# Differential attention's score rows combined by GpSimd in two operations, not by VectorE in one

## The chip, the core and the metric

The kernel runs on one core of a Trainium2 chip. The core has five engines, each with its own queue of instructions that it takes strictly in order: TensorE (PE in the profile; its weight loads are PEld), VectorE (DVE), ScalarE (ACT), GpSimd (POOL) and SyncE (SP), which issues most DMAs. They meet through semaphores. The metric is the device time of one execution in microseconds (us).

## The reference, cut to what matters

The program is a backbone of two layers over 1024 latent tokens and 256 context tokens, width 1024, float32. Each layer normalizes its input, projects it into four groups of heads (a state-space mixer, an mLSTM, differential attention, gated linear attention), joins them by an output projection and adds a squared-ReLU MLP. The change lies in differential attention. Each of its 4 heads makes two maps of scores; their softmaxes are subtracted, with a learned factor lam, before the values are summed:

```
s = einsum('bqhmd,bkhmd->bhmqk', qb, keys)      # m = 0, 1: two score maps
pr = softmax(s, axis=-1)
w = pr[:, :, 0] - lam * pr[:, :, 1]
return einsum('bhqk,bkhv->bqhv', w, vals)
```

Queries are latent tokens against all 1280 keys, and, in the first layer only, context tokens against the 256 context keys.

## The kernel before

The attention is a generator, `da_mix` (lines 453 to 594). It works on blocks of 128 queries, which I call score rows: 8 per head over 1280 keys, and in layer 0 also 2 per head over 256 keys. That is 40 score rows in layer 0 and 32 in layer 1. For one score row:

- `scores` (line 478) takes the map m = 1 first and then m = 0. Per map TensorE makes up to three pieces of scores, of 512, 512 and 256 keys (line 488, tile daps in PSUM). VectorE copies each piece to SBUF with its sign turned and takes its minimum in the same instruction (line 489, tile das). Line 498 joins the three minima. ScalarE makes the exponentials in place and their sum (line 500).
- The SBUF tile of a map has its own tag: two buffers for m = 1 and four for m = 0 (line 483, `bufs=4 - 2 * m`).
- `combine` (line 503) makes a factor r1 of 128x1 (lines 506 and 507: -lam times the sum of map 0 over the sum of map 1) and then S0 + r1 * S1 in place of S0 (line 508). It is put off: the list `late` runs it when the third score piece of the next row has been laid out (line 490).
- `values` (line 513) takes two score rows at a time: TensorE transposes blocks of the combined S0 into PSUM (line 529, tile dapt), ScalarE copies them to SBUF (line 530), and TensorE multiplies them with the values (line 520, tile dapo). `finish` (line 540) normalizes and writes the head's result to DRAM (tile mix).

Line 1497 of the main function mixes three such generators: the attention, a quarter as many steps of the mLSTM (`ml_mix`, lines 694 to 884), and the first half of the output projection (`p_out`, line 1467). In `p_out` ScalarE scales a PSUM result (line 1481, tile pg, one buffer) and GpSimd adds it to the residual (line 1482, tile xo). Lines 1446 and 1458 are VectorE's share of splitting operands into a high and a low part, lines 767, 771, 812, 839 and 853 VectorE's or GpSimd's share of the mLSTM. The transposes of the attention and the output projection share two PSUM banks in this stage (line 1487, `wo="b", dat="b"`).

The order in which an engine gets its instructions is not the order of the code: the framework lays the whole program out ahead by its own estimates, and adds the semaphore waits that the tiles ask for. A change in one instruction can so move others on every engine.

Of the kernel before, what the change touches and what calls it, by code (L numbers as in the profile page):

```python
# [17 lines left out]
ALU = mybir.AluOpType  # L18
# [434 lines left out]
def da_mix(env, l, st, V, lamv, lam_init, normg, bones, out_cb, need_ctx):  # L453
# [4 lines left out]
    v, g, act, pe = nc.vector, nc.gpsimd, nc.scalar, nc.tensor  # L458
    with tc.tile_pool(name=f"dam{l}", bufs=1, reuse_waits="tile") as P:
# [18 lines left out]
        def scores(Q, K, qt, k1, rs):  # L478
            S, sm = {}, {}
            late_at = 2  # L480
            npc = (k1 + 511) // 512
            for m in (1, 0):
                s = S[m] = P.tile([128, T], F32, tag="s%d" % m, name="das", bufs=4 - 2 * m)
                pm = P.tile([128, 4], F32, tag="pm", name="dapm", bufs=6)
                for i in range(npc):
                    a, b = 512 * i, min(k1, 512 * i + 512)
                    p = env.bank("das2" if i == 2 else "das", "daps")
                    pe.matmul(p[:, 0:b - a], Q[m][:, 128 * qt:128 * qt + 128], K[m][:, a:b], start=True, stop=True)  # L488
                    v.tensor_scalar(s[:, a:b], p[:, 0:b - a], -1.0, None, op0=ALU.mult, op1=ALU.min, accum_out=pm[:, i:i + 1])  # L489
                    if not late_at:  # L490
                        while late:
                            late.pop(0)()
                    late_at -= 1
                    yield 1
                nm = pm
                if npc > 1:
                    nm = P.tile([128, 1], F32, tag="nm", name="danm", bufs=6)
                    v.tensor_reduce(nm, pm[:, 0:npc], axis=AX.X, op=ALU.min)  # L498
                sm[m] = P.tile([128, 1], F32, tag="sm", name="dasm", bufs=6) if m else rs
                act.activation(s[:, :k1], s[:, :k1], AF.Exp, bias=nm[:, 0:1], scale=-1.0, accum_out=sm[m])  # L500
            tiles.append(S[0])

            def combine():

                r1 = P.tile([128, 1], F32, tag="rs", name="dars", bufs=6)
                v.reciprocal(r1, sm[1])
                v.tensor_scalar(r1, r1, nlam, sm[0], op0=ALU.mult, op1=ALU.mult)
                v.scalar_tensor_tensor(S[0][:, :k1], S[1][:, :k1], r1, S[0][:, :k1], op0=ALU.mult, op1=ALU.add)
            late.append(combine)
            while len(late) > 1:  # L510
                late.pop(0)()
# [1202 lines left out]
```

## Time and profile before

| | us |
|---|---|
| median of 3 runs | 3652.22 (3648.07 to 3656.89) |
| profiled execution | 3661.21 |
| its span, first to last instruction | 3659.4 |
| TensorE busy / VectorE busy / GpSimd busy | 3389.7 / 2168.1 / 453.0 |
| mean granted clock of TensorE | 0.951 of full speed |

Busy shares are means over stages with different limits, so what bounds one stage is read from that stage's own stretch of time. The attention stage of layer 0 lies between 633 and 975 us from the span's start and that of layer 1 between 2550 and 2857 us. Idle time is put down to what ended it; where several instructions were awaited, to the one that came last by the profile.

### The profile page before, as it was taken

The numbers are of one execution on the slowest core, as the hardware profiler recorded it, in microseconds if no ns is written. First come the engines' busy times: TensorE is split into PE (matmuls) and PEld (weight loads), VectorE is DVE, ScalarE is ACT, GpSimd is POOL, SyncE is SP. The second block draws the span as 40 slices with busy tenths as digits, with TensorE's granted clock in tenths as the row PEclk, the third lists the DMA queues.
The fourth block names the chain that finished last, engine by engine and source line by source line (L and its number), as shares of the span: only waits on it lengthen the run. The fifth ranks groups of instructions, "written<-read, shape, count | busy, mean of one in ns | idle before, by whom it ended". The sixth has DMA issues, their size and how long they took to land. (4 is left out here: it accounts for less than half of the span.)

```text
span 3659.4 us, 58369 instructions
## 1 busy us (share of the span) xinstructions
PE 3389.7 (93%) x22794; PEld 2687.6 (73%) x22794; DVE 2168.1 (59%) x5431; ACT 1301.5 (36%) x2453; POOL 453.0 (12%) x520
## 2 busy tenths in 40 slices
PE   6999998898789999999999798988889899999998
PEld 3867767676657888888888476867676578888885
DVE  9664655888659855455554647465888443333334
ACT  4223435666542121212112522445676322222222
POOL 2131221223100000000000123131222000000000
PEclk8989988899899999999999899998999899999999
DMA  6674325655451222222111365315654511111112
GB/s 222 238 225 150 119 79 171 201 186 158 163 179 60 95 87 80 74 76 76 64 41 38 108 199 167 119 59 173 198 179 139 168 41 49 50 47 52 46 52 75
DMA packets 233977, 430.54 MB, mean 118 GB/s; under 512 B 47414, under 2 KB 135910, under 8 KB 233446
## 3 DMA queue, kind: packets, MB, share of 16 engines
q1 hardware_dynamic: 192806, 381.03, 32.0%
q10 hardware_dynamic: 35520, 30.52, 2.6%
q0 software_dynamic: 5376, 15.28, 1.2%
q8 instruction: 179, 2.93, 0.3%
q14 instruction: 96, 0.79, 0.1%
HBM read 316.88 MB, written 109.86 MB: 117 GB/s over the span
## 5 line engine op out<-in xcount | busy, mean ns | idle before, releaser
L1563 DVE SCALAR_TENSOR_TENSOR X<-m2p,mods,X 128x256 f32<-128x256 f32 (+1 forms) x512 | 345.4, 683 | 345.2 <-PE m2p L1127 344.7
L1116 ACT CAST whi<-raw 128x1024 fp32r<-128x1024 f32 x182 | 191.1, 1050 | 916.2 <-PE m2p L1126 634.9
L1125 PE MATMUL m2p<-hidhi,whi 128*128 128x512 f32 (+1 forms) x1280 | 473.5, 372 | 2.0 <-DVE X L1563 1.3
L1125 PE MATMUL m1p<-h2hi,whi 128*128 128x512 f32 (+1 forms) x1280 | 472.6, 370 | 0.2 <-ACT h2hi L1210 0.2
L1127 PE MATMUL m2p<-hidhi,wlo 128*128 128x512 f32 (+1 forms) x1280 | 471.9, 370 | 0.8 <-DVE wlo L1117 0.8
L1126 PE MATMUL m2p<-hidlo,whi 128*128 128x512 f32 (+1 forms) x1280 | 472.7, 369 | 0.0
L1126 PE MATMUL m1p<-h2lo,whi 128*128 128x512 f32 (+1 forms) x1280 | 471.0, 368 | 0.0
L1127 PE MATMUL m1p<-h2hi,wlo 128*128 128x512 f32 (+1 forms) x1280 | 470.9, 368 | 0.0
L1117 DVE TENSOR_TENSOR wlo<-raw,whi 128x1024 fp32r<-128x1024 f32 x182 | 224.6, 1234 | 321.8 <-ACT whi L1116 303.8
L1125 PEld LDWEIGHTS m2p<-hidhi,whi 128*128 128x128 f32 x1280 | 241.4, 189 | 59.1 <-issue 9.1
L1125 PEld LDWEIGHTS m1p<-h2hi,whi 128*128 128x128 f32 x1280 | 241.0, 188 | 46.4 <-ACT whi L1116 4.2
L1127 PEld LDWEIGHTS m2p<-hidhi,wlo 128*128 128x128 f32 x1280 | 241.0, 188 | 46.3 <-issue 3.4
L1126 PEld LDWEIGHTS m2p<-hidlo,whi 128*128 128x128 f32 x1280 | 241.4, 189 | 41.8 <-issue 2.2
L1126 PEld LDWEIGHTS m1p<-h2lo,whi 128*128 128x128 f32 x1280 | 241.2, 188 | 40.6 <-DVE h2lo L1211 0.7
L1127 PEld LDWEIGHTS m1p<-h2hi,wlo 128*128 128x128 f32 x1280 | 241.0, 188 | 40.3 <-issue 0.4
L1125 PE MATMUL zp<-hhi,whi 128*128 128x512 f32 (+1 forms) x664 | 258.8, 390 | 11.3 <-ACT zst L1238 9.6
L1126 PE MATMUL zp<-hlo,whi 128*128 128x512 f32 (+1 forms) x664 | 255.7, 385 | 8.6 <-DVE hlo L1206 8.1
L1127 PE MATMUL zp<-hhi,wlo 128*128 128x512 f32 (+1 forms) x664 | 255.9, 386 | 0.0
L489 DVE TENSOR_SCALAR_CACHE_REDUCE das<-daps 128x512 f32<-128x512 f32 (+1 forms) x400 | 226.4, 588 | 44.8 <-PE daps L488 42.2
L1577 DVE TENSOR_TENSOR rl<-rl,m1p 128x256 f32<-128x256 f32 (+1 forms) x160 | 100.8, 630 | 172.2 <-ACT rl L1576 172.0
L500 ACT ACTIVATE das<-das,danm 128x1280 f32<-128x1280 f32 x128 | 174.2, 1362 | 51.4 <-DVE danm L498 51.0
L1125 PE MATMUL zp<-whi,hhi 128*128 128x256 f32 x624 | 183.6, 295 | 5.4 <-ACT whi L1116 5.2
(459 smaller groups left out, 6483.6 us busy)
## 6 DMA issues: line engine op xcount, KB each, us to landing
raw<-w SPq DMA_DIRECT2D x136, 512.0 KB
adaw<-ada_w SPq DMA_DIRECT2D x96, 512.0 KB
whl<-wsp SPq DMA_DIRECT2D x80, 512.0 KB
wsp<-whl SPq DMA_DIRECT2D x32, 512.0 KB
raw<-wz SPq DMA_DIRECT2D x30, 512.0 KB
daqk<-da_st SPq DMA_DIRECT2D x24, 640.0 KB
mlE<-ml_rows SPq DMA_DIRECT2D x16, 640.0 KB
xn<-xo SPq DMA_DIRECT2D x72, 128.0 KB
```

What stands on the lines that cost most here:

```text
L489: v.tensor_scalar(s[:, a:b], p[:, 0:b - a], -1.0, None, op0=ALU.mult, op1=ALU.min, accum_out=pm[:, i:i + 1])
L500: act.activation(s[:, :k1], s[:, :k1], AF.Exp, bias=nm[:, 0:1], scale=-1.0, accum_out=sm[m])
L1116: nc.scalar.copy(hi, raw)
L1117: nc.vector.tensor_tensor(lo, raw, hi.bitcast(F32), op=ALU.subtract)
L1125: pe.matmul(out, ah, bh, start=i == 0, stop=False)
L1126: pe.matmul(out, ah, bl, start=False, stop=False)
L1127: pe.matmul(out, al, bh, start=False, stop=i == n - 1)
L1563: nc.vector.scalar_tensor_tensor(X[b][:, m], p[:, :n], mod(l, 5, s)[:, m:m + 1], X[b][:, m], op0=ALU.mult, op1=ALU.add)
L1577: nc.vector.tensor_tensor(rl[:, :n], rl[:, :n], p[:, :n], op=ALU.mult)
```

## The change

Line 508 is replaced by two instructions of GpSimd: the first multiplies S1 by r1 in place, the second adds it to S0. The factor r1 stays on VectorE. All lines behind move down by one (line 529 becomes 530, line 1446 becomes 1447, and so on).

```
                 v.reciprocal(r1, sm[1])
                 v.tensor_scalar(r1, r1, nlam, sm[0], op0=ALU.mult, op1=ALU.mult)
-                v.scalar_tensor_tensor(S[0][:, :k1], S[1][:, :k1], r1, S[0][:, :k1], op0=ALU.mult, op1=ALU.add)
+                g.tensor_scalar(S[1][:, :k1], S[1][:, :k1], r1, None, op0=ALU.mult)
+                g.tensor_tensor(S[0][:, :k1], S[0][:, :k1], S[1][:, :k1], op=ALU.add)
             late.append(combine)
```

The framework's order differs on all engines in the two stages. Three places follow; in the rows a name's number tells one tile from another, and a wait names the engine whose semaphore is awaited (DMAHW: a DMA).

First, GpSimd near the beginning of layer 0's attention stage, before:

```order
L1482 TENSOR_TENSOR xo_6965<-xo_6965,pg_6986 128x256 [waits DMAHW7_49,DMAHW4_49,Activation_49]
L1482 TENSOR_TENSOR xo_7068<-xo_7068,pg_7089 128x256 [waits DMAHW5_49,DMAHW1_49,Activation_49]
L1482 TENSOR_TENSOR xo_7176<-xo_7176,pg_7197 128x256 [waits DMAHW3_49,DMAHW1_49,Activation_49]
L1482 TENSOR_TENSOR xo_7275<-xo_7275,pg_7296 128x256 [waits DMAHW6_49,DMAHW3_49,Activation_49]
L1482 TENSOR_TENSOR xo_7376<-xo_7376,pg_7397 128x256 [waits DMAHW7_49,DMAHW1_49,Activation_49]
L1482 TENSOR_TENSOR xo_7463<-xo_7463,pg_7484 128x256 [waits DMAHW7_49,DMAHW5_49,Activation_49]
```

And with the change, at the same place:

```order
L1483 TENSOR_TENSOR xo_6968<-xo_6968,pg_6989 128x256 [waits DMAHW6_49,DMAHW3_49,Activation_49]
L768 TENSOR_TENSOR mlE_7261<-mlE_7261,mlcm_7002 128x1280 [waits DMAHW7_49]
L1483 TENSOR_TENSOR xo_7072<-xo_7072,pg_7093 128x256 [waits DMAHW5_49,DMAHW1_49,Activation_49]
L508 TENSOR_SCALAR das_7031<-das_7031,dars_7176 128x1280 [waits DVE_49]
L509 TENSOR_TENSOR das_7057<-das_7057,das_7031 128x1280 [waits PE_49,Pool_49]
L1483 TENSOR_TENSOR xo_7181<-xo_7181,pg_7202 128x256 [waits DMAHW3_49,DMAHW0_49,Activation_49]
L508 TENSOR_SCALAR das_7151<-das_7151,dars_7311 128x1280 [waits DVE_49]
L509 TENSOR_TENSOR das_7210<-das_7210,das_7151 128x1280 [waits PE_49,Activation_49,Pool_49]
L1483 TENSOR_TENSOR xo_7280<-xo_7280,pg_7301 128x256 [waits DMAHW7_49,DMAHW3_49,Activation_49]
L508 TENSOR_SCALAR das_7275<-das_7275,dars_7434 128x1280 [waits DVE_49]
L509 TENSOR_TENSOR das_7320<-das_7320,das_7275 128x1280 [waits PE_49,Pool_49]
```

GpSimd had the additions of line 1482 and now and then an operation of the mLSTM; now a pair of lines 508 and 509 stands between nearly every two of them, and waits for VectorE's line 507 (tile dars).

Second, VectorE in layer 0, around the factor of one score row, before:

```order
L507 TENSOR_SCALAR dars_7306<-dars_7306,nlam_6698,dark_6804 128x1 [waits DVE_49,Activation_49]
L791 SCALAR_TENSOR_TENSOR mlC_7320<-mlC_7320,mlal_6647,mlpu_7327 128x65 [waits PE_49]
L1458 TENSOR_TENSOR whl_7277<-raw_7278,whl_7277 128x512 [waits DMAHW5_49,DMAHW2_49,Activation_49]
L508 SCALAR_TENSOR_TENSOR das_7205<-das_7147,dars_7306,das_7205 128x1280 [waits DVE_49]
L489 TENSOR_SCALAR das_7314,dapm_7315<-daps_7334 128x256
L791 SCALAR_TENSOR_TENSOR mlC_7319<-mlC_7319,mlal_6647,mlpu_7354 128x65 [waits PE_49]
L498 TENSOR_REDUCE danm_7337<-dapm_7315 128x1 [waits DVE_49]
L791 SCALAR_TENSOR_TENSOR mlC_7320<-mlC_7320,mlal_6647,mlpu_7358 128x65 [waits PE_49]
L1458 TENSOR_TENSOR whl_7378<-raw_7379,whl_7378 128x512 [waits DMAHW6_49,DMAHW5_49,Activation_49]
L489 TENSOR_SCALAR das_7409,dapm_7410<-daps_7411 128x512
```

With the change:

```order
L507 TENSOR_SCALAR dars_7311<-dars_7311,nlam_6698,dark_6805 128x1 [waits Activation_49]
L498 TENSOR_REDUCE danm_7343<-dapm_7321 128x1 [waits DVE_49]
L489 TENSOR_SCALAR das_7415,dapm_7416<-daps_7417 128x512 [waits Pool_49]
L772 TENSOR_TENSOR mlkw_7221<-mlkn_7006,mlE_7261 128x10x64 [waits DMAHW7_49,Activation_49]
L1459 TENSOR_TENSOR whl_7282<-raw_7283,whl_7282 128x512 [waits DMAHW2_49,DMAHW1_49,Activation_49]
L792 SCALAR_TENSOR_TENSOR mlC_7326<-mlC_7326,mlal_6647,mlpu_7333 128x65 [waits PE_49]
L489 TENSOR_SCALAR das_7415,dapm_7416<-daps_7428 128x512
L792 SCALAR_TENSOR_TENSOR mlC_7326<-mlC_7326,mlal_6647,mlpu_7364 128x65 [waits DVE_49,PE_49]
L489 TENSOR_SCALAR das_7415,dapm_7416<-daps_7431 128x256
```

Before, line 508 freed the tile das_7147 in VectorE's own order, and line 489 could write the next map 1 (das_7409) without a wait for another engine. Now line 507 releases GpSimd's pair on das_7151, whose buffer the line 489 that writes das_7415 needs: it waits for GpSimd, with one short instruction between the two.

Third, TensorE at the end of layer 0's attention stage, behind the last score piece, before:

```order
L529 MATMUL dapt_11195<-ident_67,das_10995 128x128 [waits DVE_49,PE_49]
L529 MATMUL dapt_11195<-ident_67,das_10995 128x128 x3
L520 MATMUL dapo_10261<-dawT_11194,davt_6657 64x128 [waits Activation_49]
L857 MATMUL mlpt_11110<-ident_67,mlhs_11092 128x128 [waits DVE_49]
L857 MATMUL mlpt_11110<-ident_67,mlhs_11092 128x128
L529 MATMUL dapt_11202<-ident_67,das_11129 128x128 [waits DVE_49,PE_49]
L529 MATMUL dapt_11202<-ident_67,das_11129 128x128 x3
L529 MATMUL dapt_11209<-ident_67,das_10995 128x128 [waits PE_49]
L529 MATMUL dapt_11209<-ident_67,das_10995 128x128 x3
L529 MATMUL dapt_11216<-ident_67,das_11129 128x128 [waits Activation_49]
```

With the change:

```order
L530 MATMUL dapt_11235<-ident_67,das_11033 128x128 [waits PE_49,Pool_49]
L530 MATMUL dapt_11235<-ident_67,das_11033 128x128
L858 MATMUL mlpt_11148<-ident_67,mlhs_11130 128x128 [waits DVE_49]
L858 MATMUL mlpt_11148<-ident_67,mlhs_11130 128x128
L530 MATMUL dapt_11235<-ident_67,das_11033 128x128 x2
L521 MATMUL dapo_10292<-dawT_11234,davt_6657 64x128 [waits Activation_49]
L530 MATMUL dapt_11242<-ident_67,das_11168 128x128 [waits PE_49,Pool_49]
L530 MATMUL dapt_11242<-ident_67,das_11168 128x128
L858 MATMUL mlpt_11194<-ident_67,mlhs_11176 128x128 [waits DVE_49]
L858 MATMUL mlpt_11194<-ident_67,mlhs_11176 128x128
```

The transposes of the last two score rows (the first and the second tile das here) waited for VectorE and now wait for GpSimd; what follows them in the queue is nearly the same.

## Rows read from the trace of the kernel before

**Rows 1.** The page, busy time, share of the span and instructions of each engine.

```profile
PE 3389.7 (93%) x22794; PEld 2687.6 (73%) x22794; DVE 2168.1 (59%) x5431; ACT 1301.5 (36%) x2453; POOL 453.0 (12%) x520
```

**Rows 2.** The view by windows, both attention stretches: busy us of each engine.

```profile
core 0: us, PE busy (x) PEld busy (x) DVE busy (x) ACT busy (x) POOL busy (x), PEclk, DMA share, GB/s
633.00:975.00 342.00, 297.02 (x2535) 230.66 (x2536) 275.53 (x924) 221.61 (x497) 82.54 (x76) 0.91 0.54 176
2550.00:2857.00 307.00, 271.33 (x2299) 209.79 (x2298) 251.25 (x796) 204.82 (x428) 71.79 (x62) 0.91 0.54 173
```

**Rows 3.** TensorE's waits in the two stretches: us in total, times, longest.

```profile
PE daps L488 <- DVE das L489: 22.1, 18, 5.7
PE dapt L529 <- DVE das L508: 4.1, 3, 2.6
...
PE daps L488 <- DVE das L489: 11.9, 9, 9.0
PE dapt L529 <- DVE mlrsu L62: 3.0, 2, 2.7
```

**Rows 4.** VectorE's groups by shape, line 508: count, busy us, mean ns, idle before.

```profile
L508 DVE SCALAR_TENSOR_TENSOR das<-das,dars 128x1280 f32<-128x1280 f32 x64 | 104.0, 1626 | 0.4
L508 DVE SCALAR_TENSOR_TENSOR das<-das,dars 128x256 f32<-128x256 f32 x8 | 6.4, 811 | 0.1
```

**Rows 5.** GpSimd's groups by shape over the span, those nearest to the pair.

```profile
L1482 POOL TENSOR_TENSOR xo<-xo,pg 128x256 f32<-128x256 f32 x72 | 64.6, 898 | 281.7 <-ACT pg L1481 263.8 <-DMA raw<-wo 9.0 <-ACT mlrsy L59 5.5
L947 POOL TENSOR_TENSOR glkh<-glkh,glk 128x1280 f32<-128x1280 f32 x4 | 11.7, 2928 | 56.4 <-ACT glkh L946 56.4
L321 POOL TENSOR_SCALAR s5y<-s5y 128x320 f32<-128x320 f32 x8 | 3.8, 479 | 15.8 <-ACT s5y L320 15.6
L916 POOL MEMSET glrst<- 128x1281 f32 x2 | 2.3, 1167 | 0.1
```

**Rows 6.** Timeline, VectorE's and GpSimd's instructions from 717.6: start, us.

```profile
717.68 3.13 DVE L508 SCALAR_TENSOR_TENSOR das<-das,dars 128x256 f32<-128x256 f32 x1
721.86 0.48 DVE L508 SCALAR_TENSOR_TENSOR das<-das,dars 128x256 f32<-128x256 f32 x1
...
717.62 2.91 POOL L797 TENSOR_TENSOR mlab<-mlqT,mlab 128x1280 f32<-128x1280 f32 x1 [0.54 <-PE dapt L529]
```

**Rows 7.** VectorE's groups in the two stretches, lines 1446 and 853.

```profile
L1446 DVE TENSOR_TENSOR ml<-mr,mh 128x256 fp32r<-128x256 f32 x20 | 10.4, 536 | 3.3 <-ACT mh L1445 3.3
L853 DVE TENSOR_TENSOR mlhs<-mlhs,mlrsy 128x256 f32<-128x256 f32 x9 | 4.3, 481 | 0.1
...
L1446 DVE TENSOR_TENSOR ml<-mr,mh 128x256 fp32r<-128x256 f32 x16 | 9.1, 588 | 1.4 <-ACT mh L1445 1.4
L853 DVE TENSOR_TENSOR mlhs<-mlhs,mlrsy 128x256 f32<-128x256 f32 x8 | 3.3, 416 | 0.2
```

**Rows 8.** Lines 1446 and 1482 alone: ns min/median/max, and a waiter for 1482.

```profile
L1446 DVE TENSOR_TENSOR ml<-mr,mh x56: 407/422/3118, 640.1 to 2901.1; 128x256 fp32r<-128x256 f32 x40, 128x512 fp32r<-128x512 f32 x16
...
L1482 POOL TENSOR_TENSOR xo<-xo,pg x72: 718/732/2048, 650.4 to 2783.6; 128x256 f32<-128x256 f32 x72
...
  ACT pg L1481: 2.5, 3
```

**Rows 9.** VectorE's groups over the span, score pieces and joined minima.

```profile
L489 DVE TENSOR_SCALAR_CACHE_REDUCE das<-daps 128x512 f32<-128x512 f32 x256 | 172.1, 684 | 32.9 <-PE daps L488 30.4 <-PE dapt L529 2.1
L498 DVE TENSOR_REDUCE danm<-dapm 128x1 f32<-128x3 f32 x128 | 18.9, 148 | 0.0
```

**Rows 10.** Timeline at the end of both stretches: last combinations and the transposes behind.

```profile
972.22 1.55 DVE L508 SCALAR_TENSOR_TENSOR das<-das,dars 128x1280 f32<-128x1280 f32 x1
973.92 2.88 PE L529 MATMUL dapt<-ident,das 128*128 128x128 f32 x12 [2.62 <-DVE das L508]
...
2839.53 1.55 DVE L508 SCALAR_TENSOR_TENSOR das<-das,dars 128x1280 f32<-128x1280 f32 x1
2841.23 1.72 PE L529 MATMUL dapt<-ident,das 128*128 128x128 f32 x7 [2.75 <-DVE mlrsu L62]
```

## The prediction

> **What bounds the kernel now.** I read the page's busy shares first, then the busy times in the two stretches of the attention stage, then TensorE's waits there, and last the single instructions. [rows 1]: TensorE is busy 93% of the span, VectorE 59%, GpSimd 12%. The average hides the stage that the change touches. In the two stretches of [rows 2], 342 and 307 us, which hold all 72 combinations (40 and 32), TensorE is busy 568 of 649 us, VectorE 527 (81%) and GpSimd 154 (24%). TensorE is the bound and VectorE is close behind. Of TensorE's 81 us of idle time [rows 3] shows 22.1 + 11.9 = 34 us as score matmuls that wait for VectorE's evacuation of an earlier score bank, and 4.1 + 3.0 = 7 us as transposes behind a combination (the 3.0 stands under line 62, but the timeline in [rows 10] has the combination there). These 41 us are all that a lighter VectorE could give back: the ceiling of a gain, 1.1% of the time.
>
> **What is removed.** VectorE loses 64 instructions of 1280 columns, 104.0 us, and 8 of 256 columns, 6.4 us [rows 4]: 110 of its 527 us.
>
> **What is added.** GpSimd gets 72 pairs. The second half of a pair is a two-input operation, for which [rows 5] has the same shape (line 947): 2.93 us; for 256 columns line 1482's shape, 0.73 us by its median [rows 8]. A tensor_scalar of 1280 columns doesn't stand in the trace. Bounds: not under the memset of 1281 columns, 1.17 us, which reads nothing; not over the two-input 2.93. The nearest row is line 321, a tensor_scalar of 320 columns, 0.48 us; 960 further columns at the memset's 1167/1281 = 0.91 ns give 1.35 us, which I take (0.42 for 256 columns). A combination is then 1.35 + 2.93 = 4.28 us instead of 1.55 (between 4.10 and 5.86), and GpSimd gets 64 x 4.28 + 8 x 1.15 = 283 us more: 437 of 649 us, 67% instead of 24%. It doesn't become the bound by its sum; what it costs is latency and what it does to VectorE. Four terms.
>
> **Tails, +5.5 us.** At the end of each layer's stage nothing is left beside the last combination: [rows 10] shows it at 972.22 and 2839.53, and the transposes start 0.15 us after its end, TensorE having stood idle 2.62 and 2.75 us. The third order below shows that the next work of TensorE behind them is in its queue, not beside them. Each tail grows by 4.28 - 1.55 = 2.7 us, on the path that sets the end.
>
> **The score buffer, +21 us.** The tile that a combination frees (the row m = 1, two buffers, line 483) is written by VectorE two score rows later. Before, both instructions stand in VectorE's own order and the wait costs nothing. Now that line 489 waits for GpSimd, and VectorE is in order: behind it wait the other score pieces (0.68 us each [rows 9]), the maxima that ScalarE's exponentials need, and the mLSTM pieces. The order shows 65 such waits. I laid durations from the trace on what stands between line 507 (which releases the combination) and the waiting line 489: a mean of 4.3 us over the 57 wide ones, with many short ones. The second order below has one where only line 498 lies between (0.15 us [rows 9]): VectorE stands there for about 4.1 us. Summed over all, the places shorter than the combination (30 of 65) lack 41 us (36 at the lower price, 104 at the upper). VectorE was idle 649 - 527 = 122 us here anyway, and some of that falls into the same places; I count half, 21 us.
>
> **The lock between GpSimd and VectorE, and what relief remains, -11 us.** [rows 6]: a combination of 256 columns that usually takes 0.48 us took 3.13 us from 717.68, and ended when GpSimd's 2.91 us from 717.62 were over; the next one, with GpSimd idle, took 0.48. So a VectorE instruction with two inputs in SBUF stands while GpSimd reads. About 200 others of this kind remain in the two stretches. What they lose now: line 1446 has means of 536 and 588 ns against a median of 422 ([rows 7, 8]), 0.14 us; line 853 has 481 and 416 ns, 0.03 us; I take 0.08, at 24% GpSimd. With 67% (2.8 times as often) and longer pieces (mostly 2.93 us where line 1482's are 0.9; 1.3 times the leftover) that is 0.29, or 0.21 more, times 200: +42 us on VectorE (bounds: 0.03 as base gives 16; every meeting paid in full, 67% of a mean leftover of 1.04 us less the 0.08, gives 124). VectorE ends with 527 - 110 + 42 = 459 us, 13% less. Of the 34 us that TensorE waits for its scores I let a third come back: -11 us.
>
> [...]
>
> **Queueing behind a combination, +5 us.** GpSimd's line 1482 now often stands behind a pair in its queue; pg has one buffer, so ScalarE's next line 1481 waits for it, and that holds a bank that the transposes share. Now it costs ScalarE 2.5 us in 3 waits [rows 8]. One evacuation comes per 8 to 9 us, longer than a combination, so I take 5 us (0 to 20).
>
> The order answers the longer latency in part: TensorE's transposes of the combined tile wait for GpSimd at most places, and stand about as far or farther behind the scores than before. So I charge nothing for them outside the tails.
>
> **Sum.** 5.5 + 21 - 11 + 5 = +20 us on the profiled execution, 3661.2 us (span 3659.4 and 1.8 around it): 3682. The median of the runs is 3652.2, 9 us below that execution; I forecast 3673 us.
>
> **Rivals.**
> - *Relief wins (faster).* VectorE at 81% is what TensorE waits for most in this stage, and the order was laid out anew with the lighter VectorE. Then most of the 34 us come back, the waits for the buffer fall into idle time, and only the tails stay: -34 + 5.5 = -28 us, 3624; with half of it -11, 3641. Against it: lines 489 alone, with their matmuls, still make TensorE and VectorE alternate through two banks, and the 65 new waits sit in the same instructions.
> - *Hidden (no change).* The half of the shortfall that I count also falls into VectorE's 122 idle us, the relief is a little less: 5.5 + 5 - 11 = 0 us, 3652.
> - *The lock takes all (clearly slower).* The mechanism is the one of 717.68: each meeting paid in full puts 124 us on VectorE where 110 were taken, and the buffer waits count in full, 41 us. VectorE is then at 541 + 41 = 582 us of 649, and half of the added 55 us reaches TensorE, with 41 of waits counted only once: about 27 + 21 + 5.5 + 5 = +58 us, 3710; with a tensor_scalar at 2.93 us and the shortfall of 104, up to +100, 3752. It decides once the mean excess of the 200 instructions passes about 0.5 us.
>
> **Chances.** My forecast (slower by 8 to 50 us) 0.42; the lock 0.18; hidden 0.18; relief 0.22. About 0.2%, 7 us, is what a measurement of this kernel can tell from no change: slower 0.60, same 0.18, faster 0.22. The forecast's own range is 3660 to 3700; the range that is to hold 8 times in 10 takes in half of the relief and most of the lock: 3630 to 3735.
>
> **What would show it.** In the profile after: GpSimd near 437 us busy in the two stretches, pairs of 4.2 to 4.4 us; a tensor_scalar near 1.35 us; line 489 with idle time put down to line 509 on GpSimd, some 20 to 60 us in total (step two); lines 1447, 1459, 768 and 854 with means up by 0.2 to 0.3 us, not by 0.6 (step three); transposes idle about 5.4 us behind each last combination (step one); VectorE's busy time in the stage about 459 us. I am wrong if TensorE's idle time in the two stretches falls below 81 us, or if the stretches don't change while GpSimd is at 67%; and the mechanism is wrong, whatever the time, if no line 489 waits for GpSimd.

## The result, and the profile after

The changed kernel takes 3851.8 us (median of four runs, 3845.6 to 3855.6) where the kernel before takes 3651.9: 1.054 times as long, interval 1.053 to 1.056, or 200 us more. The forecast was 3673 us, and the end of the range, 3735 us, is passed by far. The profiled execution took 3845.6 us, its span is 3843.5 us.

In the two profiled executions the difference is 184 us (that of the kernel before took 3661 us, 9 more than its median), and all of it lies in the two attention stretches. Taken from the first score matmul to the last addition of line 551 (550 before) they were 350 and 306 us long and are 449 and 393; what lies outside them is the same to 2 us. The windows of the kernel before by these bounds (the columns are those of [rows 2]):

```profile
633.00:983.00 350.00, 304.24 (x2602) 236.09 (x2602) 276.72 (x930) 225.18 (x505) 82.54 (x76) 0.91 0.54 177
2545.00:2851.00 306.00, 271.93 (x2293) 209.81 (x2294) 251.88 (x811) 202.75 (x423) 71.79 (x62) 0.90 0.54 174
```

and of the changed kernel:

```profile
630.00:1079.00 449.00, 338.46 (x2604) 256.09 (x2602) 306.65 (x890) 227.29 (x505) 293.40 (x156) 0.81 0.43 138
2641.00:3034.00 393.00, 298.36 (x2287) 227.20 (x2286) 253.51 (x776) 202.19 (x421) 270.64 (x126) 0.82 0.42 135
```

Three things are to be read from these four rows. GpSimd is busy 564 us, 410 more and not 283. VectorE, rid of 110 us, is busy 560 us instead of 529. And the 186 us divide for TensorE into 125 us more idle time (80 before, 205 now) and 61 us more busy time for the same matmuls: the granted clock, 0.91 and 0.90 before, is 0.81 and 0.82.

GpSimd's groups by shape answer to the price that I built from [rows 4, 5]:

```profile
L508 POOL TENSOR_SCALAR das<-das,dars 128x1280 f32<-128x1280 f32 x64 | 227.7, 3558 | 113.5 <-DVE dars L507 51.6 <-DVE danm L498 33.7 <-DVE mldn L834 10.2
L509 POOL TENSOR_TENSOR das<-das 128x1280 f32<-128x1280 f32 x64 | 187.7, 2933 | 3.6
L508 POOL TENSOR_SCALAR das<-das,dars 128x256 f32<-128x256 f32 x8 | 7.4, 921 | 16.4 <-DVE dars L507 13.0 <-DVE mlms L58 3.4
```

The addition is the 2.93 us foretold. The multiplication takes 3.56 us where I took 1.35; it is dearer than the two-input operation of 2.93 us that I had set as its upper bound.

VectorE's groups in the second stretch (count, busy us, mean ns, idle before) answer to [rows 7, 9]:

```profile
L489 DVE TENSOR_SCALAR_CACHE_REDUCE das<-daps 128x512 f32<-128x512 f32 x128 | 85.3, 685 | 79.0 <-POOL das L509 48.9 <-PE daps L488 20.6 <-PE dapt L530 9.5
L1447 DVE TENSOR_TENSOR ml<-mr,mh 128x256 fp32r<-128x256 f32 x16 | 15.2, 968 | 1.5 <-ACT mh L1446 1.5
L854 DVE TENSOR_TENSOR mlhs<-mlhs,mlrsy 128x256 f32<-128x256 f32 x8 | 8.8, 1100 | 0.3
L58 DVE TENSOR_SCALAR mlms<-mlms 128x4 f32<-128x4 f32 x8 | 8.7, 1094 | 0.1
```

Line 58 before:

```profile
L58 DVE TENSOR_SCALAR mlms<-mlms 128x4 f32<-128x4 f32 x8 | 1.5, 184 | 0.0
```

Line 1447 went from 588 to 968 ns, line 854 from 416 to 1100, and an instruction on four elements per partition takes 1.09 us, 184 ns before. The timeline shows why; VectorE's instructions first, then GpSimd's (start, us):

```profile
1058.67 2.76 DVE L64 TENSOR_TENSOR mlrsy<-mlrsy,mlrsu 128x4 f32<-128x4 f32 x1
...
2921.52 3.38 DVE L58 TENSOR_SCALAR mlms<-mlms 128x4 f32<-128x4 f32 x1
2928.60 3.47 DVE L63 TENSOR_SCALAR mlrsu<-mlrsu 128x4 f32<-128x4 f32 x1
...
1058.53 2.88 POOL L509 TENSOR_TENSOR das<-das 128x1280 f32<-128x1280 f32 x1
...
2921.36 3.52 POOL L508 TENSOR_SCALAR das<-das,dars 128x1280 f32<-128x1280 f32 x1
2928.53 3.51 POOL L508 TENSOR_SCALAR das<-das,dars 128x1280 f32<-128x1280 f32 x1
```

Each begins beside an addition or a multiplication and ends with it: the picture of [rows 6], now many times. Line 64 has two inputs in SBUF; lines 58 and 63 are of the form tensor_scalar and have one. I took each VectorE instruction of the two stretches that stands alone in a row of the timeline and subtracted what its group (line, operation, shape) usually takes, the tenth percentile; the excess over 0.1 us, added up, I call VectorE's lengthening. It was 27.6 us in 33 instructions and is 150.0 us in 87. None of the 770 that began while GpSimd stood idle is among them, and line 489, which reads PSUM, never is (685 ns, 684 before).

The waits of the changed kernel over the span (us, times, longest), to be held against [rows 3] and the last row of [rows 8]:

```profile
PE daps L488 <- DVE das L489: 103.2, 45, 6.9
DVE das L489 <- POOL das L509: 85.9, 25, 7.0
PE dapt L530 <- POOL das L509: 42.5, 15, 5.6
ACT pg L1482 <- POOL xo L1483: 23.8, 8, 5.4
```

TensorE's 34 us of score waits are 103; line 489 waits 86 us for GpSimd, and transposes wait 42.5 us for it, a wait that did not exist.

### The profile page after: what moved, and what is told of

It reads as the page before. It is cut to its first block, busy times and chain, and to the rows that moved or that the text cites. A ratio compares the mean times of both kernels' runs of the same rounds, so it can differ in the third digit from the quotient of the medians.

```text
span 3843.5 us, 58566 instructions
## 1 busy us (share of the span) xinstructions
PE 3445.8 (90%) x22794; PEld 2721.2 (71%) x22794; DVE 2199.2 (57%) x5359; ACT 1304.1 (34%) x2453; POOL 861.1 (22%) x664
## 3 DMA queue, kind: packets, MB, share of 16 engines
q8 instruction: 179, 2.93, 0.3%
## 5 line engine op out<-in xcount | busy, mean ns | idle before, releaser
L489 DVE TENSOR_SCALAR_CACHE_REDUCE das<-daps 128x512 f32<-128x512 f32 (+1 forms) x400 | 225.2, 589 | 162.9 <-POOL das L509 85.9
L488 PE MATMUL daps<-daqk,daqk 128*128 128x512 f32 (+1 forms) x400 | 169.6, 486 | 107.4 <-DVE das L489 103.2
L508 POOL TENSOR_SCALAR das<-das,dars 128x1280 f32<-128x1280 f32 (+1 forms) x72 | 235.1, 3265 | 129.9 <-DVE dars L507 64.6
```

The costliest lines, as they stand in the source:

```text
L508: g.tensor_scalar(S[1][:, :k1], S[1][:, :k1], r1, None, op0=ALU.mult)
```

## The experiments

Three theories. *Price*: the forecast failed because the multiplication costs 3.56 us. *Lock*: VectorE stands for as long as the GpSimd instruction that it meets, and that alone makes the loss. *Buffer*, or late release: VectorE and TensorE wait for the result of a long combination. Ratios are to the kernel before, run on the same chip; the edits are cut to the lines that change.

**A constant in place of r1.**

```diff
-g.tensor_scalar(S[1][:, :k1], S[1][:, :k1], r1, None, op0=ALU.mult)
+g.tensor_scalar(S[1][:, :k1], S[1][:, :k1], -0.25, None, op0=ALU.mult)
```

> The multiplication of line 508 takes the constant -0.25 in place of the per-partition scalar r1; the scaling by r1 is left out of the computation. Everything else is as in the changed kernel. It asks whether the 3.5 us of the multiplication come from its per-partition scalar, and what the time is once a combination costs GpSimd what I had predicted. If the per-partition scalar is what is dear: the multiplication of 1280 columns falls from 3.52 to about 1.35 us, the combination to 4.3 us. Price theory (the forecast failed because of that price alone): the time comes to the forecast, 3660 to 3700 us. Lock theory (the forecast failed because VectorE stands for the whole of nearly each GpSimd instruction that it meets): VectorE's lengthening of about 122 us shrinks only with GpSimd's added time, 283 for 428 us, to about 80 us, and the time stays well above the forecast, 3740 to 3790 us. If the multiplication stays at 3.5 us, the price is that of any tensor_scalar of this size, and the time stays at 3850 us.

3806 us (1.041, 1.039 to 1.043), where I had expected 3850 for an unchanged price.

```profile
L508 POOL TENSOR_SCALAR das<-das 128x1280 f32<-128x1280 f32 x64 | 223.2, 3488 | 91.2 <-ACT das L500 89.4 <-ACT mlrsy L59 1.7
```

The scalar's kind is not what is dear. But this row's waits show something that I had not meant: without r1 the pair starts behind the exponential (line 500), the odd tile comes free earlier, and line 489's waits for GpSimd fall from 85.9 to 7.9 us. So 152 us of loss remain with hardly a wait for the buffer, at a lengthening of 163 us: against the buffer theory as the main cause.

**A second operation.**

```diff
-... r1, None, op0=ALU.mult)
+... r1, 0.0, op0=ALU.mult, op1=ALU.add)    # two_op
+... r1, 1.0, op0=ALU.mult, op1=ALU.mult)   # mult_mult
```

> Line 508 gets a second operation that adds 0.0 after the multiplication by r1; the order of all instructions on all engines stays word for word that of the changed kernel. The constant run showed that the per-partition scalar is not what makes the multiplication dear (3.49 us with a constant). Line 321, a tensor_scalar with two operations, takes 0.41 us for 256 columns and 0.46 for 320, where line 508 takes 0.92 for 256. If a single operation is what is dear: the multiplication falls from 3.52 to 1.2 to 1.4 us and the combination to 4.2 us, with nothing else changed. Lock theory: GpSimd's added time falls from 428 to about 280 us and VectorE's lengthening with it, 122 to about 80 us: 3750 to 3800 us. Price theory: down to the forecast, 3660 to 3700 us. If the price stays at 3.5 us, the time stays at 3850 us.

> Line 508 with a second multiplication by 1.0 in place of the addition of 0.0; the order of all instructions stays that of the changed kernel. If any second operation makes the instruction cheap: 1.39 us for 1280 columns and about 3726 us in all. If it is the addition: 3.5 us or more, and 3850 us.

3725.9 us (1.020, 1.019 to 1.022) and, one run, 3723.5 us. The multiplication with an added 0.0, and with a second multiplication:

```profile
L508 POOL TENSOR_SCALAR das<-das,dars 128x1280 f32<-128x1280 f32 x64 | 89.0, 1390 | 111.3 <-DVE dars L507 46.2 <-DVE danm L498 36.5 <-DVE mldn L834 10.2
```

```profile
L508 POOL TENSOR_SCALAR das<-das,dars 128x1280 f32<-128x1280 f32 x64 | 88.9, 1389 | 112.1 <-DVE dars L507 43.1 <-DVE danm L498 37.5 <-DVE mldn L834 11.6
```

1.39 us, close to my 1.35, with VectorE's, ScalarE's and GpSimd's instructions in the same order. Both second operations make the instruction cheap, and the price is worth 126 of the 200 us. The lock theory's range was too high: GpSimd's shorter work took more than its share of the loss with it (the lengthening fell from 150 to 97 us, line 489's waits to 39). The price theory fails as well, since 74 us stay where I had forecast 20.

**GpSimd busy without reading.** Five memsets of the odd tile and half a one of the even tile in place of the pair, so that nothing is combined; then the same with a memset of r1 ahead.

```diff
-g.tensor_scalar(S[1][:, :k1], S[1][:, :k1], r1, None, op0=ALU.mult)
-g.tensor_tensor(S[0][:, :k1], S[0][:, :k1], S[1][:, :k1], op=ALU.add)
+[g.memset(r1, 0.25)]                                  # no_lock_late only
+[g.memset(S[1][:, :k1], 0.25) for _ in range(5)]
+g.memset(S[0][:, 0:k1 // 2], 0.25)
```

> GpSimd's two operations become five memsets of the odd tile of 1280 columns and one of half of the even tile: about 5.5 times 1.17 = 6.4 us per combination, as long as the pair of the changed kernel (6.45 us), on the same tiles and so with the same waits, but reading nothing from SBUF; the combination is left out of the computation. Lock theory: VectorE's long instructions (line 61 with 1.05 us for 4 elements) go back to their usual 0.16 us, VectorE's busy time in the two stretches falls from 561 to about 440 us, and most of the loss is gone: 3680 to 3740 us. Buffer theory (line 489 waiting for a long GpSimd combination is what costs): the 86 us of waits of line 489 for GpSimd remain, and the time stays at 3780 to 3850 us.

> The memsets of the run before (five of the odd tile, one of half of the even tile; the combination is left out), with a memset of r1 ahead of them, so that they can start only after line 507, as the changed kernel's combination does; in the run before they could start right after the exponential. It asks what the waits for the odd buffer cost with a combination of 6.5 us that holds VectorE less. Buffer theory: line 489 waits 60 to 100 us for GpSimd again and the time goes back to 3720 to 3800 us. Lock theory: within 25 us of the run before, 3640 to 3690 us.

3657.2 us (1.001, 1.000 to 1.003) and 3660.8 (1.002, 1.001 to 1.004), with GpSimd as busy as in the changed kernel (544 and 547 us in the stretches). That is more of the loss gone than the lock theory asked for, but both runs leave open what took it: the memsets start right behind the exponential in both (nothing makes the tile's memsets wait for r1's), line 489 waits only 16 and 12 us, so release and lock went together. Nor is the lock gone, though the name of the run says so: the lengthening is 73 and 90 us.

**The same, chained to r1.** A copy of r1 ahead of the memsets ties their start to r1, and a thin addition behind them ties the release of both tiles to the end of the chain, as the pair does; once with five memsets, once with three.

```diff
+g.tensor_scalar(S[1][:, 0:1], r1, 1.0, None, op0=ALU.mult)
+[g.memset(S[1][:, :k1], 0.25) for _ in range(5)]      # short_chain: range(3)
+g.tensor_tensor(S[0][:, 0:k1:128], S[0][:, 0:k1:128], S[1][:, 0:k1:128], op=ALU.add)
```

> In the two memset runs the memsets of the odd tile began right after its exponential and not after line 507, because nothing tied them to r1. Here a copy of r1 into one column of the odd tile stands ahead of the five memsets, and an addition of every 128th column of the two tiles behind them, so that the odd tile comes free and the transposes may start only some 6.2 us after line 507, as in the changed kernel, with GpSimd reading almost nothing. The combination is left out of the computation. If the late release is what costs (buffer theory): line 489 waits 60 to 100 us for GpSimd, transposes wait too, and the time is 3720 to 3800 us, though VectorE is lengthened less. If the lock alone made the loss: 3655 to 3690 us, as in the two memset runs.

> The run with the chained memsets with three memsets of the odd tile in place of five: 0.23 + 3 x 1.17 + 0.23 = 4.0 us from line 507 to the release, near the 4.36 us of the pair with two operations (4.28 in the forecast). The combination is left out of the computation. Late release alone, at the price of the forecast: by my forecast 21 + 5.5 + 5 - 11 = about +20 us, 3665 to 3685; if the release is what makes most of the 73 us: 3700 to 3730 us; if the release is hidden at this length and only longer ones cost: 3635 to 3660 us.

Five: 3713.7 us (1.018, 1.015 to 1.021), +62 us. Three: 3656.5 us (1.002, 1.001 to 1.003), +7 us. The waits with five:

```profile
DVE das L489 <- POOL das L510: 49.5, 41, 4.9
PE dapt L531 <- POOL das L510: 32.3, 22, 3.1
```

So a late release costs time without the pair's reading, and an earlier one is nearly paid for by VectorE's relief. How late they were I had from the sums of the parts, 6.2 and 4.0 us; in the timelines other GpSimd instructions stand between the memsets, and the release comes 9.0 and 5.0 us after line 507 by the median. The changed kernel's comes after 6.9 us and two_op's after 4.8. So the five memsets release later than the change does and lose 62 us, not 200; the three release about as two_op does and lose 7 us, not 74. The orders of the instructions differ between these runs. The lock is smaller here (51 and 34 us), and the timeline shows whom it spares:

```profile
898.52 0.15 DVE L61 TENSOR_TENSOR mlrsu<-mlrsy 128x4 f32<-128x4 f32 x1
898.71 0.16 DVE L62 TENSOR_TENSOR mlrsu<-mlrsu,mlms 128x4 f32<-128x4 f32 x1
898.90 1.23 DVE L63 TENSOR_SCALAR mlrsu<-mlrsu 128x4 f32<-128x4 f32 x1
900.17 0.16 DVE L64 TENSOR_TENSOR mlrsy<-mlrsy,mlrsu 128x4 f32<-128x4 f32 x1
...
895.28 4.83 POOL L509 MEMSET das<- 128x1280 f32 x4
```

Two SBUF inputs (lines 61, 62) pass beside a memset at 0.15 and 0.16 us, while line 63, a tensor_scalar with one input, stands to the end of a memset (the last of the four in the row below it). Beside the pair both kinds stand, as the first timeline shows.

**Three buffers for the odd tile**, and the control.

```diff
-s = S[m] = P.tile([128, T], F32, tag="s%d" % m, name="das", bufs=4 - 2 * m)
+s = S[m] = P.tile([128, T], F32, tag="s%d" % m, name="das", bufs=3)
```

> The changed kernel with three buffers for the odd and three for the even score tile, in place of two and four (there is no room for a fifth or sixth). The odd tile that a combination frees is then written three rows later. Buffer theory: most of line 489's 86 us of waits for GpSimd go, and the time falls to 3770 to 3810 us. Lock theory: VectorE's lengthening of 150 us stays, and the time stays at 3820 to 3850 us.

> The control for the run with three and three buffers and for the run with an idle pair: the kernel before with three even and three odd score tiles. VectorE frees the odd tile itself, so the third odd one gives nothing; the fourth even tile was hardly used if the transposes follow closely. All theories: 3645 to 3670 us.

With the change 3845.2 us (1.054, 1.052 to 1.056), on the kernel before 3661.5 (1.003, 1.002 to 1.004). Line 489 no longer waits for GpSimd at all, and nothing is won, though TensorE's score waits fall from 103 to 40 us. Part of the wait went to the transposes:

```profile
PE dapt L530 <- POOL das L509: 68.3, 22, 6.0
```

42.5 us before this edit. ScalarE's waits for GpSimd rise from 39 to 62 us as well, and the same matmuls take 18 us more at a clock of 0.80. The buffer was where the lateness showed, not what made it.

**An idle pair.** VectorE combines as in the kernel before; GpSimd runs a pair on a scratch tile (scr) that nobody needs. To make room, the even score tile has three buffers in these runs (the odd one two); the nearest control is before_three_three.

```diff
 v.scalar_tensor_tensor(S[0][:, :k1], S[1][:, :k1], r1, S[0][:, :k1], op0=ALU.mult, op1=ALU.add)
+g.tensor_scalar(scr[:, :k1], scr[:, :k1], r1, None, op0=ALU.mult)      # idle_two: r1, 0.0, mult, add
+g.tensor_tensor(scr[:, :k1], scr[:, :k1], scr[:, :k1], op=ALU.add)
```

In idle_memsets a copy of r1 into one column, five memsets and half a one stand in their place.

> The kernel before, VectorE combining as before, with three even and two odd score tiles; in the room that this frees GpSimd runs, after each line 507, the changed kernel's pair (a multiplication by r1 and an addition, of as many columns) on a scratch tile that nobody else touches. No engine waits for a result of GpSimd's pair; only the lock is added. Lock theory: VectorE's instructions with two SBUF inputs, its own combinations among them, are lengthened by 120 to 200 us, and the time rises to 3730 to 3820 us. Buffer theory: nobody waits, 3650 to 3680 us.

> The run with the idle pair (VectorE combines, GpSimd runs a pair on a scratch tile that nobody waits for, three even score tiles), with a second operation that adds 0.0, so that the multiplication takes about 1.4 us; the order of all instructions is word for word that of the idle pair. The lock alone at the price of the forecast. Lock theory: VectorE's lengthening falls with GpSimd's added time (280 for 430 us) from 168 to about 110 us, and the 190 us against the control to about 110 us: 3760 to 3790 us. By my forecast's +42 us on VectorE: 3680 to 3700 us.

> As the idle pair, but GpSimd's work on the scratch tile is a copy of r1 into one column, five memsets of 1280 columns and one of 640: 6.7 us per combination, as long as the pair, writing but reading nothing. VectorE combines as before, nobody waits for GpSimd. If the loss of the idle pair comes from GpSimd's reading while VectorE has two inputs in SBUF: nearly all of the 190 us go; only VectorE's instructions of the form tensor_scalar from SBUF to SBUF are still lengthened (some 30 us): 3660 to 3700 us. If any busy GpSimd holds VectorE: 3800 to 3850 us.

3851.2 us (1.055, 1.054 to 1.057), 3750.0 (1.027, 1.025 to 1.030) and 3713.1 (1.017, 1.015 to 1.019); the control is at 3661.5 us. The idle pair's windows:

```profile
625.00:1073.00 448.00, 341.86 (x2604) 263.79 (x2604) 349.05 (x931) 228.06 (x506) 310.20 (x156) 0.80 0.42 139
2629.00:3037.00 408.00, 309.15 (x2292) 236.12 (x2293) 323.14 (x811) 203.95 (x423) 285.54 (x126) 0.79 0.40 130
```

and the control's:

```profile
630.00:979.00 349.00, 302.51 (x2604) 236.10 (x2604) 273.42 (x930) 225.89 (x505) 78.83 (x76) 0.90 0.54 178
2538.00:2854.00 316.00, 278.01 (x2289) 212.85 (x2290) 247.93 (x811) 202.77 (x422) 71.14 (x62) 0.89 0.52 168
```

This is the clearest run: nobody waits for the pair, and the loss is 190 us, the whole of the change's; VectorE is busy 672 us for 521 in the control. The memsets of the same length lose 52 us, more than I had expected if GpSimd's reading is what costs (3660 to 3700 us) and far less than if any busy GpSimd holds VectorE (3800 to 3850). VectorE's lengthening explains part (56 us, 24 in the control), and GpSimd's own other instructions, which ScalarE and TensorE need, stand behind each chain. The 138 us between the two go with GpSimd's reading. Not all of them need come by way of VectorE: in the stretches ScalarE waits 110 us for GpSimd's other results beside the idle pair, 57 beside the memsets and 25 in the control, and no run separates the two ways. At the lower price the loss is 89 us, below the lock theory's range and far above my forecast.

**Addition alone on GpSimd.**

```diff
-g.tensor_scalar(S[1][:, :k1], S[1][:, :k1], r1, None, op0=ALU.mult)
+v.tensor_scalar(S[1][:, :k1], S[1][:, :k1], r1, None, op0=ALU.mult)
```

> VectorE does the multiplication of line 508 (one SBUF input) and GpSimd only the addition of line 509 (2.93 us). GpSimd gets 193 us more instead of 428. Price theory: with the dear half gone the time is near the kernel before, 3650 to 3700 us. Lock theory: the additions alone still hold VectorE, by about 193/428 of 122 = 55 us, and VectorE carries 72 multiplications of 0.7 to 1.4 us again (50 to 100 us): 3700 to 3770 us. Buffer theory: combinations of about 4 us, nearly as in the forecast, 3690 to 3730 us.

3732.1 us (1.021, 1.019 to 1.023); VectorE's multiplication takes 1.01 us, the lengthening is 95 us. Price alone is refuted; between lock and buffer this run doesn't tell.

**No combination.**

```diff
-g.tensor_scalar(S[1][:, :k1], S[1][:, :k1], r1, None, op0=ALU.mult)
-g.tensor_tensor(S[0][:, :k1], S[0][:, :k1], S[1][:, :k1], op=ALU.add)
+pass
```

> Neither engine combines the two score rows: lines 508 and 509 do nothing, and that part of the computation is left out. What is left is the ceiling of what taking 110 us from VectorE can give, with the order laid out anew for the lighter VectorE. By the third of TensorE's 34 us of score waits that I let come back, with the two tails of 1.5 us each gone: about 3638 us. If VectorE's load is what bounds the stage, all 34 us come back and more: 3600 to 3625 us. If the new order itself costs time, whatever GpSimd does: 3650 us or more.

3622.0 us (0.990, 0.988 to 0.992): 32 us faster. The relief is worth nearly all of the 34 us of score waits, not a third (with the transposes' 7 us I had called 41 the ceiling), and an order laid anew for the lighter VectorE costs nothing by itself.

**Shorter pieces.**

```diff
+for a in range(0, k1, 256):
+    g.tensor_scalar(S[1][:, a:a + 256], S[1][:, a:a + 256], r1, None, op0=ALU.mult)
+    g.tensor_tensor(S[0][:, a:a + 256], S[0][:, a:a + 256], S[1][:, a:a + 256], op=ALU.add)
```

> The changed kernel's combination in pieces of 256 columns: five multiplications of 0.92 us and five additions of 0.72, 8.2 us for 1280 columns in place of 6.45, so GpSimd works 64 x 1.75 = 112 us longer. Lock theory (a VectorE instruction stands until the GpSimd instruction that it meets ends): what is left of a piece is 0.4 us on average instead of 1.6, VectorE's lengthening falls from 150 to about 60 us, and the kernel gets faster although GpSimd works longer: 3740 to 3810 us. Buffer and price theory (a longer combination means longer waits): slower than the changed kernel, 3880 to 3960 us.

3902.1 us (1.069, 1.067 to 1.070). The lengthening fell further than expected, to 29 us, as in the kernel before; and the kernel got slower, as the buffer theory said. A combination is now 5 x (0.96 + 0.74) = 8.5 us:

```profile
DVE das L489 <- POOL das L510: 195.5, 42, 9.3
PE daps L488 <- DVE das L489: 140.4, 49, 9.4
```

The lock theory, as the sole cause, falls here: with the lock as small as in the kernel before, a later release (8.8 us after line 507 by the median, 6.9 in the changed kernel) goes with a loss of 249 us. How much a late release costs hangs on the order: the five chained memsets release as late, but more of VectorE's work stands between line 507 and the line 489 that waits (in layer 1 20 instructions by the median, 14 here), and line 489 waits 49.5 us there, not 195.5.

**Shorter pieces in the kernel before.**

```diff
-(g if hh else v).tensor_tensor(e, e, cm[:, d:d + 1].to_broadcast([128, NB, 128]), op=ALU.add)
+for c in range(0, NB, 2 if hh else NB):
+    ee = e[:, c:c + 2] if hh else e
+    (g if hh else v).tensor_tensor(ee, ee, cm[:, d:d + 1].to_broadcast([128, 2 if hh else NB, 128]), op=ALU.add)
```

> The kernel before, with one edit elsewhere: GpSimd's eight additions of 1280 columns in line 767 (3.38 us each) in five pieces of 256 columns each. In the trace of before VectorE instructions that begin beside one of these eight are lengthened by 13.0 us in all. Lock theory: some 9 us of them go, of which TensorE gets a third: 0 to 5 us faster, at the edge of what can be measured. If not the length of a GpSimd instruction but GpSimd's work in all counts: no change, or a few us slower.

3660.9 us (1.0025, 1.0013 to 1.0037): 8 us slower, though the lengthening fell from 27.6 to 19.0 us. But the pieces also take GpSimd 39.7 us in all where the eight additions took 27.0, so what the 9 us are worth by themselves this run doesn't tell. No run beats the kernel before and still combines the rows.

## Why the prediction was wrong, point by point

- **The multiplication's price, 1.35 us: the step that failed first.** I took it from line 321 and a memset, and bounded it above by the two-input 2.93. Line 321 has two operations, line 508 has one; I compared shapes and not the number of operations. It measured 3.56 us. That is a mis-sized term with a bound that was none, and two_op shows what it moved: 126 us.
- **The lock, +42 us on VectorE: the second.** It measured +122 us (27.6 to 150.0), at the price that I had assumed +69. My base was right: without the removed combinations (7.5 us of the 27.6) the lengthening is 20.1 us in 24 instructions, which is 0.07 over the 280 or so that can meet it. GpSimd's share, 67%, came out by luck: more work (564 us, not 437) in a longer stretch (842 us, not 649). What I mis-sized is the meeting: I took 2.8 times as many, each 1.3 times as long; there are 3.6 times as many (87), and the mean of a lengthened instruction went from 0.84 to 1.72 us. I also left out a kind: tensor_scalar from SBUF to SBUF (lines 58, 63, 601), which has one input.
- **From VectorE to TensorE.** I let the lock only eat relief, a third of 34 us. The relief without a lock is 32 us (no_combine), and the idle runs show that the lock's price is not bounded by it: 168 us of lengthening in idle_pair, 24 in its control, and 190 us of time; 94 and 89 in idle_two. The time holds the delays of GpSimd's other results too.
- **The score buffer, +21 us.** The mechanism is as stated (line 489 waits for line 509), and larger: 86 us. That a buffer would have cured it was wrong: with a third one the waits moved, to the transposes among others. These I had charged with nothing outside the tails, and they wait 42.5 us for GpSimd in the changed kernel. At the forecast's price and without the pair's reading, short_chain lost 7 us where I had expected some 20 by my sum; with the relief of 34 us in full, tails 5.5 + buffer 21 + queueing 5 - 34 = -3.
- **Tails, +5.5 us.** Right in number, and by luck. Behind the last combination of layer 0 the transposes waited 5.29 us (2.62 in [rows 10]), 2.7 more, as forecast for a pair of 4.28 us; the pair is 6.4 us long, by which my rule would have added 4.9. At the end of layer 1 TensorE waits 5.41 us (2.75 before) for line 854, which took 2.89 us beside the last addition of line 509:

```profile
1067.59 2.87 POOL L509 TENSOR_TENSOR das<-das 128x1280 f32<-128x1280 f32 x1
1070.52 0.69 PE L530 MATMUL dapt<-ident,das 128*128 128x128 f32 x2 [5.29 <-POOL das L509]
...
3026.20 0.69 PE L858 MATMUL mlpt<-ident,mlhs 128*128 128x128 f32 x2 [5.41 <-DVE mlhs L854]
```

- **Queueing, +5 us (0 to 20).** ScalarE's waits for line 1483 rise from 2.5 to 23.8 us; how much of that reaches the end is not shown. idle_memsets shows that such queueing, with the lock of a memset, is worth up to 52 us at the long chain.
- **The rival that came true** is the lock, with the price as its helper: its 3710 to 3752 us hold two_op (3726), the run with the price that I had taken. In part that is luck: the rival put 124 us more on VectorE and had it busy 582 us with the waits, and in two_op it is lengthened by 69 us more and busy 508 us. I gave it 0.18.
- **TensorE's clock** stood in no term. 61 of the 186 us are the same matmuls at a granted clock of 0.81, a mean between the two levels of 2.4 and 1.2 GHz, where it was 0.91. Over the runs it is lower where TensorE stood idle longer in the stretches: 0.92 and 0.94 with 56 us of idle time in both (no_combine), 0.86 and 0.88 with 122 (two_op), 0.77 and 0.78 with 234 (pieces). No run held the waits and changed the clock, so which part of the loss is its own is not shown.

Put together: of the 200 us the price makes 126, by lengthening both the lock and the release (two_op, in the same order). How the lock and the late release share the whole is not shown. Reading makes 138 us where nobody waits for the pair (idle_pair less idle_memsets); a release later than the change's, without reading, 62 us (memsets_chained); the two add up to the 200 measured, but by chance as far as is known: each edit lays the order anew, the idle pair lengthens VectorE's own combinations (54 us), which the change removed, and pieces loses 249 us with a lengthening of 29 us, no more than the kernel before has. What pieces shows is that the two trade against each other: a shorter GpSimd instruction holds VectorE less, a longer chain is waited for more.

The Trainium skill, SBUF — State Buffer, section "Who interferes with whom", says that a VectorE instruction with two SBUF inputs contends with a GpSimd instruction that reads SBUF, and not with one that only writes it. The rows agree: line 64 takes 2.76 us beside the addition's 2.88 above, and lines 61 and 62 take 0.15 and 0.16 us beside the memset. The same section says that tensor_scalar can enter a mode of VectorE that contends with GpSimd, when its operands meet that mode's conditions. Line 63's 1.23 us beside a memset and line 58's 3.38 us beside the multiplication agree; this is the kind that I left out.

## What to carry to other kernels

An operation moved to GpSimd costs three times: its own duration (here 6.5 us for VectorE's 1.6), the wait of whoever needs its result or its buffer, and the standing of most VectorE instructions with two SBUF inputs, or of the form tensor_scalar within SBUF, that meet it; count these instructions first. Take a price only from a row with the same operation and the same number of operations and inputs, and where none exists leave the upper bound open. Before giving a wait another buffer, ask who waits next for the same late result.

## What the runs showed of the hardware

A tensor_scalar on GpSimd with one operation takes 3.56 us for 128 x 1280 and 0.92 for 128 x 256 with a per-partition scalar, 3.49 and 0.85 with a constant; with a second operation that changes nothing (adding 0.0, multiplying by 1.0) it takes 1.39 us for 128 x 1280. The lock is mutual: in idle_pair GpSimd's multiplication takes 4.25 us on average instead of 3.56. The 25 that began beside a running combination of VectorE took 4.84 us by the median, the 14 that began beside its copy from PSUM (line 489) 3.52. A second input in PSUM is not held: line 813, with one input in PSUM and one in SBUF, began 51 times beside GpSimd's work in the changed kernel and never took over 0.43 us.
